# Both feed-forward openings reordered, twelve products of the ones tile at the beginning, and a chunk's next weight sums behind the last closing but one

## The chip, the cores and the metric

One core of one Trainium2 chip runs the whole kernel. The metric is the device time of one execution in microseconds (us); lower is better. The engines are named as in the profile: PE is TensorE's matrix multiplier, PEld its weight load, DVE is VectorE, ACT is ScalarE, POOL is GpSimd, and SP is SyncE, which only issues DMAs here.

## What is computed

The reference is one step of a decoder layer: a half-step SwiGLU feed-forward block, a mixer (causal pooling beside a Mamba-2 scan), a second half-step feed-forward block, and a last RMS norm. It is run for 512 new tokens of a prompt and for 8 single tokens with a state, 520 tokens in all.

```python
def _swiglu(x, wg, wu, wd):
    return (jax.nn.silu(x @ wg) * (x @ wu)) @ wd

h = h + 0.5 * _swiglu(_rms_norm(h, ffn1_norm), ffn1_w_gate, ffn1_w_up, ffn1_w_down)
m, p, c, s = _hybrid_mixer(_rms_norm(h, mix_norm), ...)
h = h + m
h = h + 0.5 * _swiglu(_rms_norm(h, ffn2_norm), ffn2_w_gate, ffn2_w_up, ffn2_w_down)
return _rms_norm(h, final_norm), ...
```

D_MODEL is 1024 and FFN_DIM 2816. All is float32. Outputs are the 520 tokens and the new states, among them the scan's states of the 8 single tokens (16 heads of 64 x 128 each).

## The kernel before

**Layout.** Features lie on the 128 partitions, tokens in the free dimension: h is 8 tiles (index d) of 128 x 520, and each matmul takes 260 tokens, a half. The feed-forward's hidden width is 22 tiles (index f). A float32 matmul is done in one of two ways. A plain product runs on float32 operands as they are and stands as two rows in the profile. `mm3` splits both operands into a high part of type fp32r and a rest (`split`: ACT casts the high part, L107; DVE subtracts it, L108) and makes three products, high by high, high by rest and rest by high (L117, L120, L121).

**A step f.** For each f both gate and up projection are wanted, for both halves. `Ffn.load` brings two weight tiles of 128 x 1024 into one buffer named `raw` (L255, L256). There are two such buffers, and they are handed round among all weight tiles of a feed-forward block in the order in which they are asked for: the closings' weights use them too. The four products gate and up by two halves are made from seven products (`product`, numbered 1 to 7) by a scheme like Strassen's: it needs sums of the weight tiles (s1 and s2, made by DVE at L262 to L264, then split into shi and slo "c" and "d") and differences of the inputs (xd). Some of the products are copied out of PSUM on the way (`ac`, ACT, L299). `gates` and `close` then make silu(gate) times up and split it into g.

**Openings.** The first tiles of each block (f = 0 and 1 in the first block, `ffn1`; f = 0 in the second, `ffn2`) are made by plain products (`plain`, L234), each over the inner index j = 0 to 3, while inputs still arrive. `prep_pair` makes the inputs' differences xd and splits inputs and differences into xth (ACT, L195) and xtl (DVE, L196). `scales` and `rstd` make the norm's factor: PE sums squares by a product with a tile of ones (psr, L163), ACT takes the root (L164), DVE the reciprocal (L165). `plain_out` multiplies by that factor (tg, L241), takes silu (L243) and multiplies by the other projection (L245). `behind[2]` orders the loading of f = 2 behind the tg multiplications of `plain_out(0)`.

**Chunks and closings.** The 22 tiles are done in chunks of 8, 8 and 6. At a chunk's end, `down` multiplies the chunk's g by the closing weights: for each d from 0 to 7 `load_unit` loads one weight tile (raw_2d for ffn2, two of them to a raw buffer, L113, issued by SP) and splits it (whi_2d by ACT, wlo_2d by DVE); PE makes 48 matmuls into dn; `done` scales the sum (td, DVE, L369) and adds it to h (L373). Before the closings start, `rest` has already asked for the first product of the next chunk's second tile (f = 9, and f = 17 after the second chunk), and with it for the whole `load`: its weight sums are made there too, and one quarter of its weights is copied aside (`held`) so that the raw buffer comes free. PE uses some of that tile's products between the closings.

**States.** In ffn2's closings the states of the single tokens are updated as well, one or two per d (`STATES`): POOL loads a row br (L831) and a state hs (L833), ACT makes so from br (L847, four instructions), DVE adds it to hs (L849, four instructions), POOL stores hs (L851). POOL's queue keeps this order: each load of hs waits for the store of the tile three before it.

**What sets the order.** The program's instructions are ordered for each engine by a list scheduler from dependencies and priorities when it is built. `tc.high_priority`, `tc.issue_after` and `tc.keep_in_program_order` steer it, and each engine then runs its list in order.

Of the kernel before, what the change touches and what calls it, by code (L numbers as in the profile page):

```python
# [9 lines left out]
F32 = mybir.dt.float32  # L10
F32R = mybir.dt.float32r
AF = mybir.ActivationFunctionType
# [4 lines left out]
P = 128  # L17
# [17 lines left out]
NG = 9  # L35
# [27 lines left out]
def tile_trunk_step(ctx: ExitStack, tc: tile.TileContext, ins: dict, outs: dict):  # L63
# [24 lines left out]
    eps = cst.tile([P, 1], F32, tag="eps", name="eps")  # L88
    nc.vector.memset(eps, EPS)

    def raw_pair(name):
        return wp.tile([P, 2, 1024], F32, tag="raw", bufs=2, name=f"raw_{name}")

# [66 lines left out]
    def rstd(r, acc, hs, width, name):  # L160
        ps = bank(f"psr_{name}")[:, : hs.stop - hs.start]
        for k, sq in enumerate(acc):
            nc.tensor.matmul(ps, ones, sq, start=k == 0, stop=k == len(acc) - 1)  # L163
        nc.scalar.activation(out=r[:, hs], in_=ps, func=AF.Sqrt, bias=eps, scale=1.0 / width)  # L164
        nc.vector.reciprocal(out=r[:, hs], in_=r[:, hs])  # L165

    def rstds(nx, name):
        for b, hs in enumerate(HALVES):
            rstd(nx[3], [nx[2][:, hs]], hs, D, f"{name}{b}")

# [11 lines left out]
                                 scale=v(norm, d))  # L182
        return xg

    def prep_pair(nx, gp, nb, xg, j, name):
        xth, xtl, _, _ = nx
        xd = gp.tile([P, 4, HB], F32, tag="g", bufs=nb, name=f"xd_{name}{j}")
        nc.vector.tensor_tensor(out=xd[:, 0:2], in0=xg[:, 0::2], in1=xg[:, 3:4].to_broadcast([P, 2, HB]),
                                op=ALU.subtract)
        nc.vector.scalar_tensor_tensor(out=xd[:, 2], in0=xd[:, 1], scalar=-1.0, in1=xg[:, 0], op0=ALU.mult,  # L190
                                       op1=ALU.subtract)
        nc.vector.scalar_tensor_tensor(out=xd[:, 3], in0=xd[:, 2], scalar=-1.0, in1=xg[:, 1], op0=ALU.mult,
                                       op1=ALU.subtract)
        for s, t in ((xg[:, 0:3], slice(0, 3)), (xd, slice(3, 7))):
            nc.scalar.copy(xth[:, j, t], s)  # L195
            nc.vector.tensor_tensor(out=xtl[:, j, t], in0=s, in1=xth[:, j, t].bitcast(F32), op=ALU.subtract)  # L196

    class Ffn:

# [2 lines left out]

        def __init__(self, nx, i, wx, gp, direct):
            self.nx, self.i, self.wx, self.gp, self.direct = nx, i, wx, gp, direct
            self.states = None
# [42 lines left out]
            nc.vector.tensor_tensor(out=g[:, 1], in0=tg, in1=g[:, 0].bitcast(F32), op=ALU.subtract)  # L248
            return free.ins

        def load(self, f):
            i, wx, src = self.i, self.wx, ins[f"w{self.i}gu"]
            n = f"{i}_{f}"
            raw = raw_pair(n)
            nc.sync.dma_start(out=raw[:, 0], in_=src[2 * f])  # L255
            nc.sync.dma_start(out=raw[:, 1], in_=src[2 * f + 1])  # L256
            d1 = split(raw[:, 0], 1024, f"{n}a", wp, 3, ("whi", "wlo"))
            s1 = wx.tile([P, 2, 512], F32, tag="sw", bufs=2, name=f"s1_{n}")
            s2 = wx.tile([P, 2, 512], F32, tag="sw", bufs=2, name=f"s2_{n}")
            up0 = raw[:, 1, :512].unsqueeze(1).to_broadcast([P, 2, 512])  # L260
            diag = bass.AP(up0.tensor, up0.offset - 1024, [up0.ap[0], (1536, 2), up0.ap[2]])
            nc.vector.tensor_tensor(out=s1, in0=diag, in1=up0, op=ALU.add)  # L262
            nc.vector.tensor_tensor(out=s2[:, 0], in0=s1[:, 1], in1=raw[:, 0, :512], op=ALU.add)
            nc.vector.tensor_tensor(out=s2[:, 1], in0=s2[:, 0], in1=raw[:, 0, 512:], op=ALU.add)  # L264
            e1 = split(s1.rearrange("p q c -> p (q c)"), 1024, f"{n}c", wx, 2, ("shi", "slo"))
# [11 lines left out]
        def product(self, f, p):  # L277
            js = range(KD // 2)
            if f not in self.A:
                with tc.issue_after(self.behind[f]) if f in self.behind else nullcontext():  # L280
                    self.load(f)
                n = f"{self.i}_{f}"
                self.A[f] = ps[0].tile([P, 512], F32, tag="A", bufs=2, name=f"A{n}")
                self.BE[f] = ps[0].tile([P, 2, 512], F32, tag="BE", bufs=2, name=f"BE{n}")
                self.ac[f] = [self.wx.tile([P, 2, HB], F32, tag="ac", bufs=3, name=f"ac{n}_{q}") for q in range(2)]
            if p != 1 and 4 not in self.w[f]:
                self.quarter(f, self.held[f])
            slot, dst, opens = {1: (0, 0, True), 2: (1, 1, True), 5: (3, 2, True), 6: (5, 0, False),
                                3: (2, 2, False), 7: (4, 0, False), 4: (6, 0, False)}[p]
            out = self.A[f] if dst == 0 else self.BE[f][:, dst - 1]  # L290
            (whi, wlo), k0 = self.w[f][p]
            xth, xtl = self.nx[:2]
            for j in js:
                mm3(out[:, :HB], ws(whi, k0 + j), ws(wlo, k0 + j), xth[:, j, slot], xtl[:, j, slot], opens and j == 0,
                    j == KD // 2 - 1, skip_group_check=True)
            a, c = self.ac[f]
            keep = {1: a[:, 0], 6: a[:, 1], 7: c[:, 0], 5: c[:, 1]}.get(p)
            if keep is not None:
                nc.scalar.copy(keep, out[:, :HB])  # L299
            if p == 7:  # L300
                nc.vector.tensor_tensor(out=c[:, 0], in0=c[:, 0], in1=c[:, 1], op=ALU.add)

        def gates(self, f):
# [11 lines left out]
            nc.vector.tensor_tensor(out=g[:, 1], in0=tg, in1=g[:, 0].bitcast(F32), op=ALU.subtract)  # L315

        def scales(self):
            rstds(self.nx, f"f{self.i}")

        def rest(self, before, last_chunk):  # L320
            lo = 0
# [20 lines left out]
        def step(self, f):  # L342
            if f not in self.A:
                self.product(f, 1)
            if f - 1 not in self.g and f > self.direct:
                self.product(f - 1, 4)
                self.close(f - 1)
            for p in (2, 5, 6, 3, 7) if f == KF - 1 else (5, 6, 3, 7, 2):
                self.product(f, p)
            self.gates(f)  # L350

        def down(self, c, lo, hi, after):
# [13 lines left out]
            def done(d):  # L366
                t = self.wx.tile([P, 2, HB], F32, tag="tg", bufs=2, name=f"td{self.i}_{d}_{c}")
                hd = h[:, d].rearrange("p (b t) -> p b t", b=2)
                nc.vector.scalar_tensor_tensor(out=t, in0=banks[d][:, :, :HB], scalar=-0.5,  # L369
                                               in1=self.nx[3].rearrange("p (b t) -> p b t", b=2), op0=ALU.mult,  # L370
                                               op1=ALU.mult)
                if after is None:
                    nc.vector.tensor_tensor(out=hd, in0=t, in1=hd, op=ALU.add)  # L373
                    return
# [13 lines left out]
            for d in range(first, KD):  # L388
                for _ in range(STATES[d] if self.states is not None else 0):
                    next(self.states)  # L390
                part(d, range(n))
                done(d)

        def down_by_half(self, c, lo, after, wd):
            n = KF - lo
# [49 lines left out]
    ffn_psum("ppf1")  # L445
    nx1 = new_xt(xt1, "f1")
    ffn1 = Ffn(nx1, 1, wx1, g1, 2)
    xg1 = []
    for j in range(KD // 2):
        for d in (j, j + KD // 2):  # L450
            q = slice(NVEC + d * NT if d else 0, NVEC + (d + 1) * NT)
# [4 lines left out]
            for d in (j, j + KD // 2):  # L456
                squares(nx1, wx1, d, "f1")
        ffn1.plain(0, xg1[j], j)
        prep_pair(nx1, g1, NG, xg1[j], j, "f1")
    ffn1.plain_load(1)  # L460
    with tc.high_priority():
        ffn1.scales()
    for u in range(2):
        for j in range(KD // 2):
            ffn1.plain(1, xg1[j], j, (u,))
    with tc.high_priority():
        ffn1.behind[2] = ffn1.plain_out(0)
    ffn1.plain_out(1)

    nx2, xa = [], []  # L470
# [33 lines left out]
    def fill(j):  # L504
        if not j:
            f2["ffn"].plain_load(0)
        f2["ffn"].plain(0, f2[j], j)
        prep_pair(f2["ffn"].nx, f2["xg"], 4, f2[j], j, "f2")
# [613 lines left out]
```

## Time and profile before

| | us |
|---|---|
| median of three runs | 993.21 (992.85 to 993.3) |
| profiled execution | 992.8 |
| its span, first to last instruction | 991.0 |
| PE busy | 969.8 (98%) |
| DVE busy | 800.0 (81%) |
| ACT busy | 552.8 (56%) |
| POOL busy | 87.4 (9%) |

The mean granted clock of PE is 0.997 of full. Spans and stretches below come from the one profiled execution, whose own time is 1.8 us more than its span and 0.4 us below the median. In rows of the timeline the first number is the start in us from the span's beginning, the second the time busy, and a bracket at the end gives the idle time before the row and what ended it. The profile leaves buffer numbers out, so raw_2d0, raw_2d2 and so on all stand as raw_2d.

### The profile page before, as it was taken

To read this page: it belongs to the slowest core of one execution; us is meant where nothing else is said; L and a number is where in the kernel's file an instruction comes from. 1 tells how busy PE (TensorE), PEld (TensorE's weight loads), DVE (VectorE), ACT (ScalarE), POOL (GpSimd) and SP (SyncE) were. 2 spreads that over 40 slices of the span, in tenths; PEclk is the share of its full clock that TensorE was granted. 3 is DMA by queue.
4 is the path that set the end of the run, shared out by engine and by line. 5 is a ranking of instruction groups with operands and counts; after the bars stand their busy time and mean duration, and the time that the engine had idled before them with its cause. 6 is when DMAs were issued, how large, how long until landed. Compare 5 with 4: busy or idle time off the path is not lost.

```text
span 991.0 us, 19414 instructions
## 1 busy us (share of the span) xinstructions
PE 969.8 (98%) x7852; PEld 951.0 (96%) x7852; DVE 800.0 (81%) x1295; ACT 552.8 (56%) x1011; POOL 87.4 (9%) x157
## 2 busy tenths in 40 slices
PE   7999999999999999999999999999999999999996
PEld 6899999999999999999899999899999999999995
DVE  7999656997569688788978997999967899668876
ACT  7566414664136455685668574666643566534653
POOL 0000000000000000156522000100013000120000
PEclk9999999999999999999999999999999999999998
DMA  6332322323222232262335232323246423363212
GB/s 188 121 128 95 120 86 86 128 86 129 85 86 81 91 126 85 82 206 100 124 114 186 81 125 86 113 98 128 100 117 198 162 88 127 120 181 119 96 65 87
DMA packets 42027, 114.48 MB, mean 116 GB/s; under 512 B 6408, under 2 KB 13512, under 8 KB 41936
## 3 DMA queue, kind: packets, MB, share of 16 engines
q1 hardware_dynamic: 38864, 103.78, 30.6%
q0 software_dynamic: 3072, 9.44, 3.7%
q8 instruction: 62, 1.02, 0.4%
q14 instruction: 29, 0.24, 0.1%
HBM read 105.86 MB, written 7.34 MB: 114 GB/s over the span
## 4 chain that ended last, share of the span: by engine, by line
PE 90%; DVE 5%; POOL 1%; DMA 1%; issue 1%; ACT 1%; SPq 0%; DVEq 0%; ACTq 0%
PE A L121 8%; PE A L117 8%; PE A L120 8%; PE dn L121 7%; PE dn L117 7%; PE dn L120 7%; PE BE L117 6%; PE BE L121 6%; PE BE L120 6%; PE wo L117 2%; PE wo L121 2%; PE wo L120 2%; PE P L234 2%; PE inz L117 2%; PE inz L121 2%; PE inz L120 2%
## 5 line engine op out<-in xcount | busy, mean ns | idle before, releaser
L117 PE MATMUL dn<-g,whi_1d 128*128 128x260 f32 x352 | 99.3, 283 | 0.2 <-DVE td L369 0.2
L120 PE MATMUL dn<-g,whi_1d 128*128 128x260 f32 x352 | 99.5, 283 | 0.0
L121 PE MATMUL dn<-g,wlo_1d 128*128 128x260 f32 x352 | 99.4, 283 | 0.0
L369 DVE SCALAR_TENSOR_TENSOR td<-dn,r_f 128x520 f32<-128x520 f32 x40 | 27.8, 698 | 72.7 <-PE dn L121 72.7
L121 PE MATMUL dn<-g,wlo_2d 128*128 128x260 f32 x256 | 72.5, 283 | 0.8 <-DVE wlo_2d L108 0.8
L117 PE MATMUL dn<-g,whi_2d 128*128 128x260 f32 x256 | 72.3, 282 | 0.0
L120 PE MATMUL dn<-g,whi_2d 128*128 128x260 f32 x256 | 72.3, 282 | 0.0
L117 PEld LDWEIGHTS dn<-g,whi_1d 128*128 128x128 f32 x352 | 66.1, 188 | 0.4 <-DVE td L369 0.4
L120 PEld LDWEIGHTS dn<-g,whi_1d 128*128 128x128 f32 x352 | 66.3, 188 | 0.0
L121 PEld LDWEIGHTS dn<-g,wlo_1d 128*128 128x128 f32 x352 | 66.2, 188 | 0.0
L299 ACT COPY ac<-A 128x260 f32<-128x260 f32 x123 | 45.6, 374 | 28.9 <-PE A L121 28.0
L107 ACT CAST whi_1d<-raw_1d 128x1024 fp32r<-128x1024 f32 (+1 forms) x24 | 23.5, 981 | 67.0 <-PE dn L120 54.2
L262 DVE TENSOR_TENSOR s<-raw 128x1024 f32<-128x1024 f32 x41 | 49.9, 1218 | 5.6 <-DMA raw<-in_w2gu 5.6
L234 PE MATMUL P<-xg_f,raw 128*128 128x260 f32 x192 | 45.4, 392 | 6.4 <-ACT sq_f L157 5.5
L121 PEld LDWEIGHTS dn<-g,wlo_2d 128*128 128x128 f32 x256 | 48.2, 188 | 1.0 <-DVE wlo_2d L108 1.0
L234 PEld LDWEIGHTS P<-xg_f,raw 128*128 128x128 f32 x192 | 36.9, 196 | 12.2 <-ACT sq_f L157 5.4
L117 PEld LDWEIGHTS dn<-g,whi_2d 128*128 128x128 f32 x256 | 48.3, 189 | 0.0
L120 PEld LDWEIGHTS dn<-g,whi_2d 128*128 128x128 f32 x256 | 48.2, 188 | 0.0
L117 PE MATMUL wo<-catg,whi_wo 128*128 128x260 f32 x128 | 37.2, 290 | 0.0
L117 PE MATMUL inz<-xh_mx,whi_inz 128*128 128x260 f32 x128 | 36.8, 287 | 0.1
L117 PE MATMUL inx<-xh_mx,whi_inx 128*128 128x260 f32 x128 | 36.4, 284 | 0.0
L121 PE MATMUL wo<-catg,wlo_wo 128*128 128x260 f32 x128 | 36.2, 283 | 0.0
(1341 smaller groups left out, 3936.7 us busy)
## 6 DMA issues: line engine op xcount, KB each, us to landing
raw<-in_w2gu SPq DMA_DIRECT2D x44, 512.0 KB, 4.5
raw<-in_w1gu SPq DMA_DIRECT2D x42, 512.0 KB, 4.5
raw_1d<-in_w1d SPq DMA_DIRECT2D x16, 512.0 KB, 4.5
raw_2d<-in_w2d SPq DMA_DIRECT2D x16, 512.0 KB, 4.4
raw_wo<-in_w_out SPq DMA_DIRECT2D x12, 512.0 KB, 4.9
ab<-scr_acs SPq DMA_DIRECT2D x8, 512.0 KB, 4.9
h<-in_state_ssm SPq DMA_DIRECT2D x16, 256.0 KB, 3.7
raw_inz<-in_w_in SPq DMA_DIRECT2D x8, 512.0 KB, 3.8
```

Of the source, the lines that this page charges most:

```text
L107: nc.scalar.copy(h, src)
L117: first = nc.tensor.matmul(ps, whi, xhi, start=start, stop=False, **kw)
L120: nc.tensor.matmul(ps, whi, xlo, start=False, stop=False, **kw)
L121: nc.tensor.matmul(ps, wlo, xhi, start=False, stop=stop, **kw)
L234: nc.tensor.matmul(self.banks[f, u][b][:, :HB], ws(self.raw[f][:, u], j + 4 * q), xg[:, slot[q]], start=j == q == 0, stop=j == 3 and q == ...
L262: nc.vector.tensor_tensor(out=s1, in0=diag, in1=up0, op=ALU.add)
L299: nc.scalar.copy(keep, out[:, :HB])
L369: nc.vector.scalar_tensor_tensor(out=t, in0=banks[d][:, :, :HB], scalar=-0.5, in1=self.nx[3].rearrange("p (b t) -> p b t", b=2), op0=ALU.mult,
```

## The change

The beginning of the kernel gets 12 products of `ones` with itself, into a PSUM bank of their own that nobody reads. In ffn1's opening the second part of the last `prep_pair` (the split of xd for j = 3) is put off behind the roots and behind the tg of `plain_out(0)`. In ffn2's opening the first product of f = 1 is asked for ahead of `scales`, f = 1 takes its products in another order with two of them pinned, and the sum s1 of f = 2 is made by three DMAs of POOL, two copies and one that adds, instead of DVE. In ffn2 the weight sums of f = 9 and f = 17 (s1, s2 and their splits) are no longer made in `load`, but in `sums`, called in the closings' loop behind the h add of d = 6. The raw buffer of f = 9 and f = 17 is read until then.

The diff's core (line numbers of the functions move; `queued` enters `issue_after` for several instructions):

```diff
-    def prep_pair(nx, gp, nb, xg, j, name):
+    def prep_pair(nx, gp, nb, xg, j, name, late=None):
...
-        for s, t in ((xg[:, 0:3], slice(0, 3)), (xd, slice(3, 7))):
+        def parts(s, t):
             nc.scalar.copy(xth[:, j, t], s)
-            nc.vector.tensor_tensor(out=xtl[:, j, t], in0=s, in1=xth[:, j, t].bitcast(F32), op=ALU.subtract)
+            return nc.vector.tensor_tensor(out=xtl[:, j, t], in0=s, in1=xth[:, j, t].bitcast(F32), op=ALU.subtract)
+
+        parts(xg[:, 0:3], slice(0, 3))
+        if late is not None:
+            late.append(lambda: parts(xd, slice(3, 7)))
+            return None
+        return last.ins, parts(xd, slice(3, 7)).ins
...
-        def load(self, f):
+        def load(self, f, first, then, by_dma):
...
-            d1 = split(raw[:, 0], 1024, f"{n}a", wp, 3, ("whi", "wlo"))
+            with queued(*first):
+                d1 = split(raw[:, 0], 1024, f"{n}a", wp, 3, ("whi", "wlo"))
+            if f in self.held and self.states is not None:
+                self.w[f] = {1: (d1, 0), 2: (d1, 4)}
+                self.lazy[f] = lambda: self.sums(f, n, src, raw, d1, by_dma)
+                return
+            with queued(*then):
+                self.sums(f, n, src, raw, d1, by_dma)
+
+        def sums(self, f, n, src, raw, d1, by_dma):
...
-            nc.vector.tensor_tensor(out=s1, in0=diag, in1=up0, op=ALU.add)
+            if by_dma:
+                low = src[2 * f + 1][:, :512].unsqueeze(1).to_broadcast([P, 2, 512])
+                nc.gpsimd.dma_start(out=s1[:, 0], in_=src[2 * f][:, :512])
+                nc.gpsimd.dma_start(out=s1[:, 1], in_=src[2 * f + 1][:, 512:])
+                nc.gpsimd.dma_start(out=s1, in_=low, accum_op=ALU.add)
+            else:
+                nc.vector.tensor_tensor(out=s1, in0=diag, in1=up0, op=ALU.add)
...
-            for p in (2, 5, 6, 3, 7) if f == KF - 1 else (5, 6, 3, 7, 2):
-                self.product(f, p)
+            if f == self.early:
+                for p in (6, 7, 5, 4, 3, 2):
+                    self.product(f, p, p in (5, 4))
+            else:
+                for p in (2, 5, 6, 3, 7) if f == KF - 1 else (5, 6, 3, 7, 2):
+                    self.product(f, p)
...
-                done(d)
+                added = done(d)
+                if d == KD - 2 and hi + 1 in self.lazy:
+                    with tc.issue_after(added):
+                        self.lazy.pop(hi + 1)()
...
+    warm = bank("warm")
+    for _ in range(12):
+        nc.tensor.matmul(warm[:, :P], ones, ones, start=True, stop=True)
...
-        prep_pair(nx1, g1, NG, xg1[j], j, "f1")
+        prep_pair(nx1, g1, NG, xg1[j], j, "f1", late if j == KD // 2 - 1 else None)
...
     with tc.high_priority():
-        ffn1.behind[2] = ffn1.plain_out(0)
+        free = ffn1.plain_out(0)
+        with queued(root, free):
+            late.pop()()
+        ffn1.behind[2] = (free,), (free,), False
...
+    f2["ffn"].early = 1
+    f2["ffn"].product(1, 1)
     with tc.high_priority():
-        f2["ffn"].scales()
-        f2["ffn"].behind[2] = f2["ffn"].plain_out(0)
+        with tc.issue_after(f2["ffn"].kept), tc.issue_after(f2["low"]):
+            f2["ffn"].scales()
+        f2["ffn"].behind[2] = (f2["last"],), (f2["ffn"].plain_out(0),), True
```

More of the change, by code (lines that the diff above doesn't have):

```diff
@@ L89, in tile_trunk_step, with queued @@
     nc.vector.memset(eps, EPS)
+    def queued(*ins):
+        stack = ExitStack()
+        for i in ins:
+            stack.enter_context(tc.issue_after(i))
+        return stack
     def raw_pair(name):
@@ L163, in rstd @@
             nc.tensor.matmul(ps, ones, sq, start=k == 0, stop=k == len(acc) - 1)
-        nc.scalar.activation(out=r[:, hs], in_=ps, func=AF.Sqrt, bias=eps, scale=1.0 / width)
+        root = nc.scalar.activation(out=r[:, hs], in_=ps, func=AF.Sqrt, bias=eps, scale=1.0 / width)
         nc.vector.reciprocal(out=r[:, hs], in_=r[:, hs])
+        return root.ins
     def rstds(nx, name):
         for b, hs in enumerate(HALVES):
-            rstd(nx[3], [nx[2][:, hs]], hs, D, f"{name}{b}")
+            root = rstd(nx[3], [nx[2][:, hs]], hs, D, f"{name}{b}")
+        return root
     def new_xt(xp, name):
@@ L191, in prep_pair @@
                                        op1=ALU.subtract)
-        nc.vector.scalar_tensor_tensor(out=xd[:, 3], in0=xd[:, 2], scalar=-1.0, in1=xg[:, 1], op0=ALU.mult,
-                                       op1=ALU.subtract)
-        for s, t in ((xg[:, 0:3], slice(0, 3)), (xd, slice(3, 7))):
+        last = nc.vector.scalar_tensor_tensor(out=xd[:, 3], in0=xd[:, 2], scalar=-1.0, in1=xg[:, 1], op0=ALU.mult,
+                                              op1=ALU.subtract)
+        def parts(s, t):
             nc.scalar.copy(xth[:, j, t], s)
-            nc.vector.tensor_tensor(out=xtl[:, j, t], in0=s, in1=xth[:, j, t].bitcast(F32), op=ALU.subtract)
+            return nc.vector.tensor_tensor(out=xtl[:, j, t], in0=s, in1=xth[:, j, t].bitcast(F32), op=ALU.subtract)
[4 more added lines that the diff above has]
+        return last.ins, parts(xd, slice(3, 7)).ins
     class Ffn:
@@ L204, in __init__ @@
             self.nx, self.i, self.wx, self.gp, self.direct = nx, i, wx, gp, direct
-            self.states = None
+            self.states = self.early = None
+            self.lazy = {}
             self.held = {CHUNKS[0] + 1: None, CHUNKS[0] + CHUNKS[1] + 1: None}
@@ L256, in load @@
             nc.sync.dma_start(out=raw[:, 1], in_=src[2 * f + 1])
-            d1 = split(raw[:, 0], 1024, f"{n}a", wp, 3, ("whi", "wlo"))
+            with queued(*first):
[7 more added lines that the diff above has]
+        def sums(self, f, n, src, raw, d1, by_dma):
+            wx = self.wx
             s1 = wx.tile([P, 2, 512], F32, tag="sw", bufs=2, name=f"s1_{n}")
@@ L261, in load @@
             diag = bass.AP(up0.tensor, up0.offset - 1024, [up0.ap[0], (1536, 2), up0.ap[2]])
-            nc.vector.tensor_tensor(out=s1, in0=diag, in1=up0, op=ALU.add)
+            if by_dma:
[5 more added lines that the diff above has]
+                nc.vector.tensor_tensor(out=s1, in0=diag, in1=up0, op=ALU.add)
             nc.vector.tensor_tensor(out=s2[:, 0], in0=s1[:, 1], in1=raw[:, 0, :512], op=ALU.add)
             nc.vector.tensor_tensor(out=s2[:, 1], in0=s2[:, 0], in1=raw[:, 0, 512:], op=ALU.add)
-            e1 = split(s1.rearrange("p q c -> p (q c)"), 1024, f"{n}c", wx, 2, ("shi", "slo"))
+            with tc.high_priority() if by_dma else nullcontext():
+                e1 = split(s1.rearrange("p q c -> p (q c)"), 1024, f"{n}c", wx, 2, ("shi", "slo"))
             e2 = split(s2.rearrange("p q c -> p (q c)"), 1024, f"{n}d", wx, 2, ("shi", "slo"))
@@ L275, in quarter, with product @@
             self.w[f][4] = split(src, 512, f"{self.i}_{f}b", wp, 3, ("whi", "wlo")), 0
-        def product(self, f, p):
+        def product(self, f, p, pin=False):
             js = range(KD // 2)
             if f not in self.A:
-                with tc.issue_after(self.behind[f]) if f in self.behind else nullcontext():
-                    self.load(f)
+                self.load(f, *self.behind.get(f, ((), (), False)))
                 n = f"{self.i}_{f}"
@@ L294, in product @@
                 mm3(out[:, :HB], ws(whi, k0 + j), ws(wlo, k0 + j), xth[:, j, slot], xtl[:, j, slot], opens and j == 0,
-                    j == KD // 2 - 1, skip_group_check=True)
+                    j == KD // 2 - 1, pin=pin and j == 0, skip_group_check=True)
             a, c = self.ac[f]
@@ L298, in product @@
             if keep is not None:
-                nc.scalar.copy(keep, out[:, :HB])
-            if p == 7:
+                self.kept = nc.scalar.copy(keep, out[:, :HB]).ins
+            if p == (5 if f == self.early else 7):
                 nc.vector.tensor_tensor(out=c[:, 0], in0=c[:, 0], in1=c[:, 1], op=ALU.add)
@@ L317, in scales @@
         def scales(self):
-            rstds(self.nx, f"f{self.i}")
+            return rstds(self.nx, f"f{self.i}")
         def rest(self, before, last_chunk):
@@ L345, in step @@
             if f - 1 not in self.g and f > self.direct:
-                self.product(f - 1, 4)
+                if f - 1 != self.early:
+                    self.product(f - 1, 4)
                 self.close(f - 1)
-            for p in (2, 5, 6, 3, 7) if f == KF - 1 else (5, 6, 3, 7, 2):
-                self.product(f, p)
+            if f == self.early:
[4 more added lines that the diff above has]
+                    self.product(f, p)
             self.gates(f)
@@ L372, in done @@
                 if after is None:
-                    nc.vector.tensor_tensor(out=hd, in0=t, in1=hd, op=ALU.add)
-                    return
+                    return nc.vector.tensor_tensor(out=hd, in0=t, in1=hd, op=ALU.add).ins
                 for b, hs in enumerate(HALVES):
@@ L447, in tile_trunk_step @@
     ffn1 = Ffn(nx1, 1, wx1, g1, 2)
-    xg1 = []
+    xg1, late = [], []
+    warm = bank("warm")
+    for _ in range(12):
+        nc.tensor.matmul(warm[:, :P], ones, ones, start=True, stop=True)
     for j in range(KD // 2):
@@ L458, in tile_trunk_step @@
         ffn1.plain(0, xg1[j], j)
-        prep_pair(nx1, g1, NG, xg1[j], j, "f1")
+        prep_pair(nx1, g1, NG, xg1[j], j, "f1", late if j == KD // 2 - 1 else None)
     ffn1.plain_load(1)
     with tc.high_priority():
-        ffn1.scales()
+        root = ffn1.scales()
     for u in range(2):
@@ L507, in fill @@
         f2["ffn"].plain(0, f2[j], j)
-        prep_pair(f2["ffn"].nx, f2["xg"], 4, f2[j], j, "f2")
+        f2["last"], f2["low"] = prep_pair(f2["ffn"].nx, f2["xg"], 4, f2[j], j, "f2")
     ps[0] = tc.alloc_tile_pool(name="ppm", bufs=8, space=PSUM, reuse_waits="tile")
```

## The prediction, on record before the changed kernel ran

> **What bounds the kernel now.** First the page's busy times, the slices and the chain.
>
> ```profile
> PE 969.8 (98%) x7852; PEld 951.0 (96%) x7852; DVE 800.0 (81%) x1295; ACT 552.8 (56%) x1011; POOL 87.4 (9%) x157
> ...
> PE   7999999999999999999999999999999999999996
> ...
> PE 90%; DVE 5%; POOL 1%; DMA 1%; issue 1%; ACT 1%; SPq 0%; DVEq 0%; ACTq 0%
> ```
>
> PE is the bound. It keeps every matmul after the change, so only its waits and its slow first stretch can be won, or new waits be added. PE's waits:
>
> ```profile
> PE P L234 <- ACT sq_f L157: 5.5, 1, 5.5
> PE A L117 <- ACT ac L299: 1.8, 2, 1.4
> PE P L234 <- DVE tg L241: 0.9, 1, 0.9
> ...
> PE dn L121 <- DVE wlo_2d L108: 0.8, 1, 0.8
> ```
>
> Each line is total, number, longest. The first is the start, which the change does not shorten. The next two are the openings, the last the closing of a chunk of ffn2. Little is to be won, so the question is what the change may add. It touches the loop of closings most, so I read DVE's timeline in ffn2's first one:
>
> ```profile
> 735.22 0.70 DVE L369 SCALAR_TENSOR_TENSOR td<-dn,r_f 128x520 f32<-128x520 f32 x1 [3.10 <-PE dn L121]
> 735.95 0.70 DVE L373 TENSOR_TENSOR h<-td,h 128x520 f32<-128x520 f32 x1
> 736.57 1.14 DVE L849 SCALAR_TENSOR_TENSOR hs<-hs,sdec,so 128x128 f32<-128x128 f32 x4
> 737.62 1.22 DVE L108 TENSOR_TENSOR wlo_2d<-raw_2d,whi_2d 128x1024 fp32r<-128x1024 f32 x1
> 740.99 0.70 DVE L369 SCALAR_TENSOR_TENSOR td<-dn,r_f 128x520 f32<-128x520 f32 x1 [2.15 <-PE dn L121]
> ```
>
> After each closing d, DVE scales it (td), adds it to h, updates a state tile (hs) and splits a weight (wlo_2d). At 735.22 this is td of d=1; the wlo_2d at 737.62 is for d=3. Then the weight load that SP issues at 738.9, and the DMA engines around it (PE, PEld, DVE, ACT, POOL busy, clock, DMA share, GB/s):
>
> ```profile
> L113 SPq DMA_DIRECT2D raw_2d<-in_w2d x2: 328/392/457, 738.9 to 739.2; - x2
> ...
> DMA to landing us min/median/max: 7.8/7.8/7.8
> ```
>
> ```profile
> 739.00:747.00 8.00, 8.00 (x69) 8.00 (x68) 3.58 (x7) 2.40 (x6) 1.69 (x4) 1.00 0.83 231
> ```
>
> This pair (d=6, 7) starts the moment wlo_2d of d=3 has ended (738.84) and takes 7.8 us, among the state stores and loads that POOL issues at 738.0, 738.5 and 740.6. Nobody waits for it: its cast runs only at 752.9.
>
> **The closings of ffn2 (the large term).** Before, the weight sums of f=9 were made before the closings, which freed its raw buffer. There are two; so SP loaded the closings' weights two pairs ahead. Now these sums stand behind the h add of d=6 (`lazy`), and raw_9 is read until then. In the changed program's semaphore waits the pairs therefore share one buffer: pair (2, 3) waits for wlo_2d of d=1, pair (4, 5) for that of d=3, pair (6, 7) for that of d=5. SP's order is the same; behind each waiting load stand only the next loads.
>
> Pair (2, 3): wlo_2d of d=1 ends before closing 0 does, and a load at 727.6 landed in 3.5 and 4.4 us; closing 2 is over 5.8 us later. No stall.
>
> Pair (4, 5): a closing is 48 matmuls at 0.12 us start to start (5.76). From the end of closing 1 to the start of closing 4 there are two closings, 11.5 us. td starts 0.15 after closing 1, wlo_2d of d=3 ends and SP issues 3.7 after that (735.22 to 738.9), which leaves 7.65. Needed: the landing, the cast (1.05, L107), the subtraction (1.22, L108), 0.15 of handing over, less 0.24 for two products that need only the cast. With 7.8, the landing of the load that stood in this very place, that is 9.98: a stall of 2.3. In chunk 2 the same load (865.6) landed in 7.4: 1.9. At the quickest landing (3.5) or the page's median (4.4) there is none.
>
> Pair (6, 7): from the end of that late subtraction PE has 46 matmuls and closing 5, 11.3 us. DVE has td, h, eight hs and wlo_2d of d=5 (747.22 to 751.89, 4.7), so 6.6 remain. In this place raw of the next f was loaded before: 5.3 us for its first half in chunk 1 (751.9), 6.9 in chunk 2 (878.65). Needed: 5.3+1.05+1.22+0.15-0.24 = 7.5, a stall of 0.9; in chunk 2 I take 6.1, between the two, 8.3 and a stall of 1.7. Bounds: 0, and 3.4 each (7.8). A second wait lies here: ACT's cast for d=6 now stands behind the state product so60 (L847), which needs POOL's br load; it landed in 4.9 and 7.0 before (750.5, 877.4). Issued some 1.4 before the weights, it is done about when they are, so I add nothing.
>
> The 24 matmuls of f=9 that stood between closings (2.9 us) come after d=7. They add no time, but were cover. DVE then has s1, two s2, two slo for f=9 behind d=6, and the sums of f=10 only behind d=7. Summing 1.14 for 1024 and 0.61 for 512 elements from closing 7's start, slo_10d ends 18.4 after it and PE wants it at 17.9: 0.5 per chunk (0 to 1.0).
>
> Gain: the 0.93 at 892.1 to 893.2 in chunk 2, where sums of f=18 (waiting for a load until 886.91) and a br load held wlo_2d of d=7. I book all of it.
>
> Sum: 2.3+1.9+0.9+1.7+1.0-0.9 = +6.9 (bounds -0.9 and about +12).
>
> **Opening of ffn1.** Two lines of PE's timeline:
>
> ```profile
> 5.46 18.37 PE L234 MATMUL P<-xg_f,raw 128*128 128x260 f32 x76 [5.46 <-ACT sq_f L157]
> ...
> 29.98 7.28 PE L234 MATMUL P<-xg_f,raw 128*128 128x260 f32 x32 [0.89 <-DVE tg L241]
> ```
>
> A plain product costs 0.439 at full speed; until about 8.1 they run at half, 1.33 over in all. The 12 products need only `ones` (memset ends at 1.0). At 128/260 of a product's columns they take 2.6 at full speed, 5.2 at half, so end between 3.6 and 6.2: before the 5.46 at which the first real product may start, or 0.7 behind. If the clock is up by then, PE reaches its inputs early: the scaled inputs of j=1 and j=2 (xg, L181, ready at 9.03 and 13.0) cost 0.1 and 0.45. The Trainium skill, "TensorE: Matmul & The Clock Gate", section "What's actually happening", has a free-running window of 3.4 us that must be busy before the full rate; the trace's switch 2.7 us after the first product agrees in size. By its free phase the 12 products might miss the switch, and this opening would win 0.3 and not 1.1. The wait for tg (1.04 over) becomes 0.75: the roots no longer stand behind the cast of j=3 (from 24.1 on), the reciprocals (3.41 at 25.90 before) run from 24.6 to 28.0, both tg (0.70) to 28.7. PE has had two products moved ahead and gets there at 27.96 instead of 28.9. The late xtl of j=3 on DVE delays slo_2d to 39.0, wanted at 39.2. Sum: 1.33-0.55+1.04-0.75 = 1.07, a gain of 1.1 (0.3 to 2.4).
>
> **Opening of ffn2.** Before: 1.53 at 638.4, 0.62 at 641.6, 0.39 at 652.4 over, 2.54. After: wlo_2a stands before xtl on DVE, so A of f=2 waits 0.5; ACT copies ac ahead of the roots, which ends the first wait; the second copy's stays (0.62); roots, reciprocals (1.78) and tg come 0.6 later, so BE of f=1 waits 0.45; shi_2c and slo_2d behind the later table load and silu cost 0.4 each. Sum 2.37, a gain of 0.2 (loss 1.2 to gain 1.0). The s add of f=2 (1.22 on DVE at 644.6) becomes three POOL DMAs, issued about 620 ahead of br and hs on POOL's queue. No accumulating DMA is in the trace; POOL's loads of 256 KB landed in 2.8 to 8.0, so copies and the accumulation end by 636, hidden by 9 us. Later, silu would wait for it.
>
> All: +6.9-1.1-0.2 = +5.6. The profiled execution took 992.8 (span 991.0 and 1.8 around it), 0.4 under the median: 998.4 there, 998.8 in the median.
>
> **Rivals.** (1) Faster: the pairs land quicker than those of before, as the load of f=10 now follows the closings. It decides at 5.5 us for pair (4, 5): below, no closing waits. Then -0.9+1.0-1.1-0.2 = -1.2, or -2.2 without the tail: about 991.5. For: 3.5 to 4.9 at 727.6 and 854.4. Against: those ran without POOL's stores and loads, which now stand as before (0.83 of the engines). The Trainium skill, "DMA: Bandwidth & Descriptors", section "Anatomy of one DMA", fits 2.0 us plus bytes over 436 GB/s; an estimate by it is 4.4 for a pair, hence this rival; the trace's 7.8 under load is against it. Chance 0.13.
>
> (2) Only pair (4, 5) is late and DVE's tail costs nothing: 2.3+1.9-0.9-1.3 = +2.0, 995.2, on the upper edge of no change. 0.2% (2.0 us) is about what a measurement of this kernel can tell. Chance 0.15, half of it within.
>
> (3) Pair (6, 7) also takes 7.8, as both may with br and hs beside them: 2.3+1.9+6.8+1.0-0.9-1.3 = +9.8, 1003. For: 7.0 and 7.3 us for br in chunk 2. Chance 0.15.
>
> (4) The openings' reorderings win nothing (clock not raised, ffn2's roots later): +6.9, up to +8, 1001. Chance 0.1.
>
> The forecast keeps 0.47. The range 993.2 to 1003.5 leaves out most of rival 1 and the end of rival 3. Faster 0.12 (rival 1), same 0.10 (half of 2, the edge of 1), slower 0.78.
>
> **What would show it.** In the profile after: PE waits "dn <- wlo_2d" or "whi_2d" of about 2 us near the start of closing 4 in both chunks, a smaller one at closing 6; SP's raw_2d loads spread over the loop, one pair at a time, where before the last was issued at 739 and 866; the chain passing through DMA and ACT there. The slice of the first products at full clock, tg's wait below 0.9. I am wrong if no dn wait is over 1 us, or if the openings move by more than 2.

## The result, and the profile after

| | before | after |
|---|---|---|
| device time, median (lowest to highest) | 993.03 us (991.83 to 993.32) | 996.93 us (996.33 to 998.21) |
| ratio to before | | 1.0043, 95% interval 1.003 to 1.0056 |
| profiled execution: time, span | 992.8, 991.0 us | 997.39, 995.5 us |

The changed kernel is slower by 0.43%, some 3.9 us in the medians and 4.5 in the spans of the two profiled executions. The page after, its busy times, PE's slices and the shares of the chain:

```profile
PE 976.7 (98%) x7876; PEld 955.3 (96%) x7876; DVE 799.8 (80%) x1294; ACT 552.9 (56%) x1011; POOL 90.1 (9%) x160
...
PE   9999999999999999999999999999999999999996
...
PE 85%; DVE 7%; DMA 4%; ACT 2%; issue 1%; SPq 1%; POOL 0%; DVEq 0%; ACTq 0%
```

PE does the same work with 24 matmul rows more (the 12 products), and its first slice is now full. The chain holds 4% of DMA where it held 1%, and less of PE: a transfer has come onto the path. Which one, PE's waits tell (total, number, longest, in us):

```profile
PE dn L127 <- DVE wlo_2d L114: 2.9, 4, 0.8
...
PE A L123 <- DVE tg L257: 0.8, 1, 0.8
...
PE A L123 <- ACT ac L331: 0.5, 1, 0.5
```

The wait of a closing for its weights, one of 0.8 before, is four of 2.9 in all: at closings 4 and 6 of chunk 1 and of chunk 2. The two waits of the openings, 1.8 for ac and 0.9 for tg before, are 0.5 and 0.8. The longest gap alone is listed, and shorter ones lie around it; measured as what start to start takes over 0.12 us per matmul, closing 4 lost 1.33 in chunk 1 and 1.58 in chunk 2, closing 6 lost 0.92 and 1.0. By the row alone, whose longest wait is 0.8, the prediction's sign of being wrong (no dn wait over 1 us) would be met; it is the sum of the gaps at closing 4, 1.33 and 1.58, that clears it. The stretch before closing 4 of chunk 1 on ACT and on DVE, and SP's loads of chunk 1's closing weights (start, duration, engine, work, and in brackets the idle time ahead and what ended it):

```profile
743.13 1.05 ACT L113 CAST whi_2d<-raw_2d 128x1024 fp32r<-128x1024 f32 x1 [6.59 <-DMA raw_2d<-in_w2d]
```

```profile
739.81 1.14 DVE L897 SCALAR_TENSOR_TENSOR hs<-hs,sdec,so 128x128 f32<-128x128 f32 x4
744.21 1.23 DVE L114 TENSOR_TENSOR wlo_2d<-raw_2d,whi_2d 128x1024 fp32r<-128x1024 f32 x1 [3.27 <-ACT whi_2d L113]
745.35 0.69 DVE L406 SCALAR_TENSOR_TENSOR td<-dn,r_f 128x520 f32<-128x520 f32 x1
```

```profile
709.01 42.01 SPq L119 DMA_DIRECT2D raw_2d<-in_w2d  x8
```

SP's eight loads now stretch over 42.01 us (29.81 before): one pair at a time. ACT stands idle for 6.59 us until the weights of d=4 land, DVE 3.27 for ACT's cast. The load that they wait for, and the window around it (busy time of PE, PEld, DVE, ACT, POOL, then clock, DMA share, GB/s):

```profile
L119 SPq DMA_DIRECT2D raw_2d<-in_w2d x2: 328/390/451, 736.3 to 736.7; - x2
...
DMA to landing us min/median/max: 6.7/7.1/7.6
```

```profile
736.00:744.00 8.00, 8.00 (x69) 7.97 (x67) 2.76 (x7) 1.41 (x3) 2.16 (x5) 1.00 0.81 221
```

Pair (4, 5) leaves at 736.3, one closing before it is wanted; its first half lands in 6.7 us and its second in 7.6, with the DMA engines at 0.81. The beginning, on PE:

```profile
1.06 5.03 PE L490 MATMUL warm<-ones 128*128 128x128 f32 x24 [1.06 <-DVE eps L89]
5.92 7.18 PE L250 MATMUL P<-xg_f,raw 128*128 128x260 f32 x32
...
24.79 3.67 PE L250 MATMUL P<-xg_f,raw 128*128 128x260 f32 x16
...
29.24 0.36 PE L123 MATMUL A<-xth_f,whi_2a 128*128 128x260 f32 x1 [0.78 <-DVE tg L257]
```

The 12 products (24 rows) fill 1.06 to 5.92, 0.46 past the 5.46 at which the first real product started before; behind them the products run at full speed.

By landmarks common to both traces (the starts of the same matmuls), the opening of ffn1 gained 0.75, the opening of ffn2 0.3, the closings of chunk 1 lost 3.2 and those of chunk 2 2.4. That makes 4.55, as the two spans say (4.5); the medians differ by less, 3.9, and the six executions of the changed kernel lie 1.9 apart.

### The profile page after: what moved, and what is told of

Its sections match the earlier page's. It is cut to its first block, busy times and chain, and to the rows that moved or that the text cites. A ratio compares the mean times of both kernels' runs of the same rounds, so it can differ in the third digit from the quotient of the medians.

```text
span 995.5 us, 19464 instructions
## 1 busy us (share of the span) xinstructions
PE 976.7 (98%) x7876; PEld 955.3 (96%) x7876; DVE 799.8 (80%) x1294; ACT 552.9 (56%) x1011; POOL 90.1 (9%) x160
## 4 chain that ended last, share of the span: by engine, by line
PE 85%; DVE 7%; DMA 4%; ACT 2%; issue 1%; SPq 1%; POOL 0%; DVEq 0%; ACTq 0%
PE A L127 8%; PE A L123 7%; PE A L126 7%; PE dn L127 6%; PE dn L123 6%; PE dn L126 6%; PE BE L127 5%; PE BE L123 5%; PE BE L126 5%; PE P L250 3%; DMA raw_2d<-in_w2d 2%; PE wo L123 2%; PE wo L127 2%; PE wo L126 2%; PE inz L123 2%; PE inz L127 2%
## 5 line engine op out<-in xcount | busy, mean ns | idle before, releaser
L113 ACT CAST whi_2d<-raw_2d 128x1024 fp32r<-128x1024 f32 (+1 forms) x18 | 18.4, 1024 | 35.6 <-DMA raw_2d<-in_w2d 22.4
```

Of the source, the lines that this page charges most:

```text
L113: nc.scalar.copy(h, src)
```

## The experiments

Theory A: with its sums late, f=9 (and f=17) keeps one of the two raw buffers, so each pair is loaded only one closing ahead and lands late. Rivals: the work that moved behind closing 7 costs it (the sums, and the 24 matmuls that stood between the closings); or ACT's order of state products and casts. Besides the times, one stretch serves as a measure that the openings don't touch: from the start of the first matmul on whi_2b (660.47 in the profile after) to that of the seventh on whi_20a (928.91), which holds both loops of closings. It is 262.84 us before and 268.45 after.

**The late sums taken out of the change.**

```
-            if f in self.held and self.states is not None:
+            if False:
```

> The changed kernel, with the weight sums of f=9 and f=17 made in load again, as before. Buffer theory (the closings wait because raw_9 and raw_17 hold one of the two raw buffers until d=6): SP's closing weights are loaded two pairs ahead again, no dn wait at closings 4 and 6, and only the openings are left, which stood 1.15 us ahead of before in the profile at f=2's last product of ffn2: about 991.9, 0.1% faster than before. The wait of 0.9 at closing 7 of the second chunk comes back. Rival (the 12 products or the sum by POOL's DMAs cost something of their own later): 993 or more.

Measured: 991.97 (991.05 to 993.09), ratio to before 0.9993 (0.9984 to 1.0001); stretch 262.66. None of the four waits at closings 4 and 6 is left; the one at chunk 2's closing 7, which before had too, is back:

```profile
PE dn L127 <- DVE wlo_2d L114: 0.6, 1, 0.6
```

All of the loss is in the late sums. The openings together are worth something between a loss of 0.1 and a gain of 1.6 us by this interval.

**The late sums alone, in the kernel of before.**

```
+            if f in self.held and self.states is not None:
+                self.w[f] = {1: (d1, 0), 2: (d1, 4)}
+                self.lazy[f] = lambda: self.sums(f, n, src, raw, d1)
+                return
...
+                if d == KD - 2 and hi + 1 in self.lazy:
+                    with tc.issue_after(added):
+                        self.lazy.pop(hi + 1)()
```

> The kernel before with one part of the change alone: the weight sums of f=9 and f=17 behind the h add of d=6. Buffer theory: all of the loss, which in the profile of the changed kernel is 3.2 us over the first chunk's end and 2.4 over the second's: 993.0+5.6 = 998.6, dn waits at closings 4 and 6 of 0.9 to 1.6 each. Rival (the loss comes from the openings' shift against POOL's state loads): clearly less than +5.

Measured: 999.33 (997.7 to 999.38), ratio 1.0062 (1.0049 to 1.0076); stretch 267.54.

```profile
PE dn L121 <- DVE wlo_2d L108: 2.2, 3, 0.8
```

Closings 4 of both chunks and 6 of chunk 1 wait as in the changed kernel. Closing 6 of chunk 2 lost 0.27 only: its pair landed quicker that time, the second half in 5.9 where the changed kernel had 6.4. The orders of PE, DVE and ACT in the first chunk's closings are those of the changed kernel, so the pair's landing decides, not its place in the order. The median is 6.6 above before, more than expected: in the profiled execution 4.7 of it lie in the stretch, 0.85 ahead of it and 0.9 outside the span (2.7 us where before had 1.8); what made these two larger stays open.

**The late sums with a buffer of their own.** The weights of f=9 and f=17 are loaded into the two tiles of the sums, which are then made in place, at the same place behind d=6; the ring of raw buffers is free for the closings.

```
+            if f in self.held and self.states is not None:
+                lo, up = (wx.tile([P, 2, 512], F32, tag="sw", bufs=2, ...) for t in ("s2", "s1"))
+                nc.sync.dma_start(out=lo..., in_=src[2 * f])
+                nc.sync.dma_start(out=up..., in_=src[2 * f + 1])
+                ...
+                self.lazy[f] = lambda: self.own_sums(f, n, lo, up, d1)
```

> The changed kernel, with the weights of f=9 and f=17 loaded into the two tiles of the weight sums (tag sw), where the sums are then made in place behind the same h add of d=6 (four adds of 512 instead of one of 1024 and two of 512). The raw buffers are both free for the closings. Order on DVE, ACT and PE in the closings stays. Buffer theory: no wait at closings 4 and 6 (1.3, 0.9 and 1.6, 1.0 us with the slower products behind them go), the tails at slo_9d and slo_10d stay (0.26 and 0.6 per chunk): 996.9-4.8 = 992.1. Rival (the lost fillers, or ACT's so products ahead of the casts, which wait for br, cost the time): waits at closings 4 and 6 stay, 995 or more.

Measured: 992.85 (992.14 to 993.98), ratio 1.0001 (0.9992 to 1.001); stretch 263.63. No closing waits for its weights, though PE's order in the closings and the lateness of the sums are those of the changed kernel. So the work that moved behind closing 7 is not the main cause. On ACT one thing differs, the state product so60 stands behind the cast of d=6 here and ahead of it in the changed kernel; but there that cast, behind so60, still waited 0.82 for its own load, and the cast of d=4 waited 6.59 for its load and for nothing of ACT's (743.13 above), so ACT's order is out too. What lateness itself costs is the tail behind closing 7: waits of 0.29 for slo_9d, 0.22 for slo_10d, 0.28 for slo_17d and 0.26 for slo_18d, 1.7 in all with the slower matmuls beside them. Against it stands the wait at chunk 2's closing 7, 1.0 before, which is gone. The stretch is the changed kernel's less the four waits (268.45-4.83 = 263.62), as expected, tails included; the 0.75 by which the median exceeds the expectation lies outside the stretch and is not explained.

**Without the state updates in the closings.**

```
-                for _ in range(STATES[d] if self.states is not None else 0):
-                    next(self.states)
```

> The changed kernel without the states' updates in ffn2's closings (new states of the single tokens aren't computed or stored; no br, hs and out_nss DMAs there). The closings' weights still share one buffer. If the waits come from loads that are slow because POOL's stores and loads run beside them: the pairs land in 3.5 to 5 us and no dn wait above 0.3 is left at closings 4 and 6, about 992. If the loads take 6 to 7 us by themselves, the waits of about 1 us stay and so does 996 or more.

This kernel leaves the new states out. Measured in one execution: 990.7 us; stretch 262.31. The pairs are still loaded one at a time, but pair (4, 5) of chunk 1 lands in 3.7 and 4.6 us, and closings 4 and 6 wait for nothing. One buffer alone is not enough for the loss, then. But two things went with the states: POOL's stores and loads beside the pair, and the hs of DVE ahead of wlo_2d. Without that hs the pair leaves 8.75 us before closing 4 begins; in the changed kernel it leaves 7.68 before closing 4 would have begun had it not waited. At the changed kernel's landing of 6.7 that earlier start alone would leave some 0.3 of the 1.33 (an estimate: 1.33 less 1.07). This run does not tell the two apart; the next does.

**The sums earlier, behind d=1.**

```
-                if d == KD - 2 and hi + 1 in self.lazy:
+                if d == 1 and hi + 1 in self.lazy:
```

> The late sums stand behind the h add of d=1 instead of d=6; everything else is the changed kernel. The buffer theory: raw_9's buffer comes free right after closing 1, so the pair (6, 7) takes it and is loaded far ahead, while the pair (4, 5) still waits for wlo_2d of d=3 as before this edit. So the waits at closing 6 (0.9 and 1.0 us) and the tails behind closing 7 (0.9 each) vanish, the waits at closing 4 (1.3 and 1.6) stay, and a wait of some 0.6 at closing 7 of chunk 2 may return, as in the kernel with the sums ahead of the closings: 992.0 + 2.9 = 994.9 us. If the price were the lateness of the sums themselves (work of VectorE behind closing 7) and not the ring, closing 4 would not wait either and the time would be 992.

Measured: 991.56 (991.19 to 992.95), ratio 0.9992 (0.9983 to 1.0001); stretch 262.73. My expectation of 994.9 failed: closing 4 does not wait, although its pair had to wait for the same subtraction as in the changed kernel and left at the same 736.4. It left 7.82 us ahead of closing 4, where the changed kernel had 7.68, and landed sooner:

```profile
L119 SPq DMA_DIRECT2D raw_2d<-in_w2d x2: 327/380/433, 736.4 to 736.7; - x2
...
DMA to landing us min/median/max: 3.8/4.2/4.6
```

And POOL tells why. First the changed kernel, then this one:

```profile
735.47 0.55 POOL L899 DMA_DIRECT2D out_nss<-hs  x1 [2.49 <-DVE hs L897]
736.01 0.54 POOL L879 DMA_DIRECT2D br<-scr_bc  x1
738.07 0.54 POOL L881 DMA_DIRECT2D hs<-in_state_ssm  x1 [1.52 <-DMA out_nss<-hs]
```

```profile
733.79 0.54 POOL L881 DMA_DIRECT2D hs<-in_state_ssm  x1 [2.88 <-DMA out_nss<-hs]
743.56 0.55 POOL L899 DMA_DIRECT2D out_nss<-hs  x1 [9.23 <-DVE hs L897]
```

The sums stand ahead of the state update on DVE, so the store of the updated state, and br and hs behind it on POOL's queue, start 8 us later, when the pair has landed. (The sums have a price of their own there: pair (2, 3) leaves 3 us later, and closing 2 loses 0.33 and 0.47 waiting for it.) This was found after the run, so it was put to a test of its own.

**The state steps moved away from the pair.** Everything as in the changed kernel, sums at d=6; the step of d=2 is made with that of d=3.

```
-STATES = (0, 1, 1, 1, 2, 1, 1, 1)
+STATES = (0, 1, 0, 2, 2, 1, 1, 1)
```

> The changed kernel, sums at d=6, all weights in the same two buffers; only the eight state steps of a chunk are spread over the closings as (0,1,0,2,2,1,1,1) instead of (0,1,1,1,2,1,1,1), so that GpSimd starts no store and no load between about 733 and 741 us, when the pair (4, 5) is on its way. If the state traffic beside it is what makes that landing slow, the pair lands in 3.8 and 4.6 us instead of 6.7 and 7.6 and the waits at closing 4 (1.3 and 1.6) go, while those at closing 6 (0.9 and 1.0, at most a little less) and the tails (0.9 each) stay: 996.9 - 2.9 = 994.0 us, 993.0 if the earlier wlo_2d of d=5 takes the waits at closing 6 away too. If a pair that has only one buffer before it lands in 7 whatever runs beside it, closing 4 waits 0.3 or more still (the pair is issued about 1 us earlier) and the time stays above 995.5.

Measured: 993.37 (992.67 to 995.13), ratio 1.0011 (1.0002 to 1.002); stretch 264.03.

```profile
742.31 0.55 POOL L899 DMA_DIRECT2D out_nss<-hs  x1 [8.38 <-DVE hs L897]
```

```profile
L119 SPq DMA_DIRECT2D raw_2d<-in_w2d x2: 328/380/433, 736.4 to 736.7; - x2
...
DMA to landing us min/median/max: 3.8/4.2/4.6
```

POOL is quiet from 733.9 to 742.3, pair (4, 5) lands in 3.8 and 4.6, and closing 4 waits in neither chunk. Closing 6 lost 0.44 in chunk 1 and nothing to be seen in chunk 2, between the two cases expected; the tails are 0.87 and 0.8. With the same work, bytes and buffers, a step moved by one closing takes back 4.4 of the 5.6 us that the stretch had lost. Not all of that is the quicker landing: the hs that moved away also stood ahead of wlo_2d on DVE. Closings 0 to 3 of this execution begin 1.08 later than in the changed kernel, so the pair that leaves at the same 736.4 leaves 8.75 us ahead of closing 4 instead of 7.68, and pair (6, 7) leaves at 749.0 instead of 750.0. At closing 4 either would have done nearly all; that the landing alone does it is shown by the experiment before, in which the lead was 7.82.

**A buffer of their own and the sums behind d=1.** The kernel of the third experiment with the edit of the fifth.

```
-                if d == KD - 2 and hi + 1 in self.lazy:
+                if d == 1 and hi + 1 in self.lazy:
```

> The kernel in which the weights of f=9 and f=17 have buffers of their own, with the sums behind the h add of d=1 instead of d=6. Buffer theory: no dn wait at closings 4 and 6 as before this edit; the waits for slo_9d, slo_10d, slo_17d, slo_18d behind closing 7 (1.1 us in all in that kernel) go, since VectorE has done the sums by then. Against its 992.85 that is 991.8; with a wait of 0.6 at closing 7 of chunk 2 come back, 992.4. If VectorE has no room for 5 us of sums between closings 1 and 4, waits for wlo_2d appear at closings 3 to 5 and it is slower than 993.

Measured: 991.33 (990.51 to 991.87), ratio 0.9988 (0.9979 to 0.9997); stretch 262.85. No dn wait of 0.3 or more and no tail: as expected and a little better. (A wait of 0.6 ahead of whi_8b, before closing 1 of chunk 1, is in this execution alone.) It has the lowest median of the kernels that do all of the work, and its interval stays just below 1; by the 0.2% at which a difference counts here it is level with before.

**Without the products of the ones tile.**

```
-    for _ in range(12):
+    for _ in range(0):
```

> The openings as changed, the sums ahead of the closings, and no product of the ones tile at the beginning. Theory: the 12 products take the slow first stretch away (1.3 to 2.5 us over full speed in the executions without them) and give back 0.5 us by ending at 5.9 instead of 5.5 and 0.5 by PE reaching its inputs early: 0.3 to 1.4 us slower than with them (991.97), so 992.3 to 993.4. Rival: the first stretch is waited off anyway at the inputs of j=1 to 3, and the 12 products win nothing: 991.8 to 992.2.

Measured: 992.09 (991.45 to 993.48), ratio 0.9996 (0.9987 to 1.0005).

**Ten of them.**

```
-    for _ in range(12):
+    for _ in range(10):
```

> The same with 10 products of the ones tile instead of 12. In the changed kernel 12 of them ran at half clock from 1.06 to 5.92, 0.41 each, and the first real product started 0.46 later than it could. Ten end at 5.1: the first product starts at 5.46. If the clock has risen by then: 0.3 to 0.5 faster than with 12, 991.5 to 991.7. Rival: the idle time of 0.3 ahead of the first product holds the clock down, and the slow first stretch comes back: 992.3 to 993.4.

Measured: 991.76 (990.47 to 992.25), ratio 0.999 (0.9981 to 0.9999). Both of these also make the sums ahead of the closings, so the kernel with 12 products to compare them with is that of the first experiment (ratio 0.9993). The intervals overlap over most of their length: the times don't tell 0, 10 and 12 products apart. The traces show where a gain would go. PE at the end of the first opening, without the products and with ten:

```profile
23.88 1.04 PE L169 MATMUL psr_f<-acc_f,ones 128*128 128x260 f32 x4
24.76 5.50 PE L250 MATMUL P<-xg_f,raw 128*128 128x260 f32 x24
```

```profile
23.87 1.04 PE L169 MATMUL psr_f<-acc_f,ones 128*128 128x260 f32 x4
24.75 3.23 PE L250 MATMUL P<-xg_f,raw 128*128 128x260 f32 x14
29.19 0.36 PE L123 MATMUL A<-xth_f,whi_2a 128*128 128x260 f32 x1 [1.22 <-DVE tg L257]
```

Two rows are one product: without the products of the ones tile 38 real products stand ahead of psr, with ten 41, with twelve 40. So the time won was filled with two or three products moved ahead (0.439 us each), and psr starts at 23.88 without and at 23.87 with ten. The root, the reciprocals and tg hang on psr, so tg comes no sooner, and PE, those products ahead, waits 1.22 for it with ten and 0.78 with twelve, where it doesn't wait without. The first matmul on shi_2d starts at 39.12 without the products, at 39.20 with ten, and at 38.70 to 39.65 in the seven executions with twelve. Thereafter the execution without them has a wait of 0.43 for whi_3a; whether that belongs to it or to that one execution stays open.

## Why the prediction was right, and where it was not

The direction, the mechanism and the places held; 998.8 was 1.9 us too much, inside the range. That it came so near is in part luck: the four waits of the closings were forecast 2.0 too large in all and the tails 0.7 too small. Point by point:

- **Pair (4, 5), forecast 2.3 and 1.9, measured 1.33 and 1.58.** The mechanism was right: the first and second experiments put the whole loss in the late sums, the third puts the waits in the buffer. The time left was right too (7.65 forecast, 7.68 measured). The term was mis-sized in its landing. The 7.8 taken from the row of before stands alike as minimum, median and maximum of two loads, and so is one landing; the changed kernel's row has two, 6.7 for the first half and 7.6 for the second, and the cast of d=4 needs the first only. With 6.7 and 6.9 (chunk 2) in place of 7.8 and 7.4 the prediction's own working gives 1.2 and 1.4.
- **Pair (6, 7), forecast 0.9 and 1.7, measured 0.92 and 1.0.** The first half landed in about 5.5 in both chunks, where 5.3 and 6.1 were taken. The wait of ACT behind so60 cost nothing, as booked: so60 ran at 753.47, and the cast still waited 0.82 for its own load.
- **Tails, forecast 0.5 per chunk, measured 0.87** (slo_9d 0.26, slo_10d 0.61; chunk 2 0.27 and 0.60). The first of the two was not in the sum.
- **Gain 0.9 at closing 7 of chunk 2: right.** The wait is not in the profile after, and it is back when the sums go ahead of the closings again. All terms of the closings: 1.33+1.58+0.92+1.0+0.87+0.87-0.93 = 5.6, where the forecast had 6.9.
- **Opening of ffn1, forecast -1.1, measured -0.75; opening of ffn2, forecast -0.2, measured -0.3.** In ffn2 the waits listed are there but smaller (0.34 for wlo_2a where 0.5 was taken, 0.38 for shi_2c and 0.21 for slo_2d where 0.4 was), and the one of 0.45 at BE of f=1 is not. For ffn1 the step that failed is the first of its sum, 1.33 won at the start less 0.55 at inputs: by the experiment without the products most of that comes back as a wait for tg, and up to shi_2d the traces have the whole gain without them too (39.99 before, 39.12 in the execution without the products): there it is the earlier root's, whose reciprocals start at 25.03 instead of 25.90.
- **The three accumulating DMAs on POOL: hidden, as forecast.** They are issued from 617.7 to 622.0, the two copies land in 3.0 us and the one that adds in 6.1, by 628.1 where the forecast allowed 636, and no wait for them shows.
- **Rival 1 (quick landings, 991.5)** was wrong for this kernel, but right in its deciding point: where the pair landed in 3.7 to 3.8 (state steps left out or moved, or sums behind d=1) closing 4 did not wait. The prediction took POOL's transfers as fixed surroundings. They are not: they follow DVE's order, and moving a state step by one closing, which shifts them and wlo_2d together, takes back most of the loss. The Trainium skill, "DMA: Bandwidth & Descriptors", section "Anatomy of one DMA", has a fit of 2.0 us plus bytes over 436 GB/s for one DMA on GpSimd's path; carried over to SP's pair, taken as one transfer, it gives an estimate of 4.4. The trace agrees where POOL is quiet (4.6), and not beside POOL's transfers (7.6), where the measurement decides.
- **Rivals 2 and 3** fall by the waits at closing 6: they are there, and about 1; rival 2 also falls by the tails, 0.87 per chunk. **Rival 4** falls half: the products of the ones tile win nothing that shows, the reordered roots do in the traces.

## What to carry to other kernels

Work that is put off keeps its inputs alive, so before it is moved, count which ring its buffer belongs to and who is next in that ring: here 5 us of vector work put off took one of two buffers from the loads of a whole loop. A load with one buffer before it has little slack (7.68 us here), so its landing counts, and here that changed from 3.8 to 6.7 us with its company: look at what other queues issue in the same 5 us, for a step moved by one place may cost less to try than a buffer. Warming an engine up pays as far as the next thing it waits for, and that was here a chain through another engine that the warm-up did not shorten.

## What the hardware showed that was not expected

- The landing of a pair of 512 KB loads that left at 736.3 was 6.7 and 7.6 us in the changed kernel, with a state store (735.47), a row load br (736.01) and a state load (738.07) of POOL beside it, and another store and row load from 741.24 on; it was 3.8 and 4.6 with POOL quiet. From 736.3 to 741.0 the DMA engines were busy 0.78 of the time in the changed kernel and moved 132 GB/s; with the state step moved away they were busy 0.64 and moved 223 GB/s. The bytes that POOL added don't explain it, since fewer bytes moved in all. The trace points to the row load. Here are each queue's packets, MB and share of the time of the 16 DMA engines from 737.4 to 739.9, first in the changed kernel, then with the state step moved (q0 is POOL's queue, which is missing where POOL is quiet; q1 is SP's):

```profile
q0 software_dynamic: 23, 0.07, 75.5%
q1 hardware_dynamic: 17, 0.07, 19.0%
```

```profile
q1 hardware_dynamic: 209, 0.79, 92.5%
```

  In these 2.5 us 0.07 MB of POOL's held three quarters of the engines' time, 1.9 us on each of the 16, and SP's pair got 17 packets through where it otherwise got 209. The store's 256 KB had moved by 737.4, and the state load was only issued at 738.07; by size and order the 0.07 MB are the 64 KB of br, which landed 5.8 us after it was issued. In chunk 2 the same 2.5 us (867.5 to 870.0) show 79.1% and 13.1%. This is read from traces; no run leaves br alone out.
- The 12 products took 4.5 to 5.3 us in different executions, and the 38 real products up to psr took 18.2, 18.5 and 19.6 in three executions without them (16.7 at 0.439 each). The slow stretch, in which rows start 0.43 apart and not 0.22, lasted 2.7 us in the profiled execution of before and 5.8 in that of the late sums alone, whose beginning is the same. The Trainium skill, "TensorE: Matmul & The Clock Gate", section "What's actually happening", calls the clock's window free-running; the spread agrees with that. One execution is too few to price a warm-up by.
